# RMSNorm with each row written twice: roots and reciprocals of several rows in one instruction, the last copies on ScalarE

## The chip, the cores and the metric

The kernel runs on one core of a Trainium2 chip. A core has several engines that work side by side, each with its own queue of instructions: VectorE (DVE in the profile), ScalarE (ACT), GpSimd (POOL) and SyncE (SP), which here only issues transfers. TensorE is not used. Sixteen DMA engines move data between the main memory (HBM) and the on-chip memory, whose 128 partitions each hold a stretch of bytes. The metric is device time in microseconds (us); lower is better.

## The reference

```
x_rep = np.repeat(x, 2, axis=1)
rms = np.sqrt((x_rep ** 2).mean(axis=-1, keepdims=True) + 1e-6)
x_norm = x_rep / rms
return (x_norm * gamma[None, None, :]).astype(np.float32)
```

`x` is 8 x 512 x 2048 in float32, 33.6 MB, and `gamma` has 2048 elements. Each of the 4096 rows is divided by the root of its mean square, multiplied by `gamma`, and written twice, one copy after the other: 67.1 MB of output.

## The kernel before

The 4096 rows are cut into eight tiles of 512 rows: a tile has K = 4 rows in each of 128 partitions. One load (`load`, line 50) brings two tiles, that is eight consecutive rows of 8 KB per partition, 8.39 MB. One store (`store`, line 53) writes one tile with every row twice, again eight rows per partition and 8.39 MB. There are four loads and eight stores, all issued by SyncE on one queue, so a store that still waits for its data holds back whatever is behind it.

One buffer `y` holds 24 rows per partition and is used as three areas of eight rows, `first`, `second` and `third`. The function `four` (line 90) works through four tiles and is called twice:

- Load n goes into rows 4 to 11 (half of `first` and half of `second`), load n + 1 into `third`.
- Tile 1 lies in the upper half of `first`. It is spread over all of `first`, to rows 0, 2, 4 and 6 from the front, and stored.
- Tile 2 lies in the lower half of `second`. It is spread over `second`, last row first, and stored.
- Tiles 3 and 4 lie in `third`. The roots of all their eight rows are taken first. Tile 3 then goes to `first`, once the store of tile 1 has read it; tile 4 is spread over `third`.

For each row, ScalarE squares it and sums the squares (`square`, line 60; the sum comes out of a second, short instruction, the accumulator's read-out), then takes the root of the mean plus `eps` (line 62). VectorE takes the reciprocal (line 67) and multiplies the row by it and by `gamma` into its place (line 68). When the four rows of a tile stand, they are copied to the odd places (`repeat`, line 75): the lower two rows by ScalarE, the upper two by VectorE. In tiles 3 and 4 too, each engine takes one copy.

The order on every engine is the program's order (`manual_schedule`, line 86). `constants` (line 109), called once between the first two loads, issues two transfers of `gamma` from ScalarE's queue, spreads it over the partitions on GpSimd and sets `eps_t` by a memset on VectorE. ScalarE's functions come in sets that have to be loaded before the first use (`ACT_TABLE_LOAD`): the profile shows one load before the first square and one before the first root, and none after.

Around the change the order is set by three things: the landing of loads 0 and 2, after which tile 1's four rows go through ScalarE and VectorE; SyncE's queue, in which the store of tile 1 stands behind the two loads; and the landing of tile 1's store, for which the multiplies of tile 3 wait.

Of the kernel before, what the change touches and what calls it, by code (L numbers as in the profile page):

```python
# [1 line left out]

# [4 lines left out]


@with_exitstack
def kernel(  # L10
    ctx: ExitStack,
    tc: tile.TileContext,
    x: bass.AP,
    gamma: bass.AP,
    out: bass.AP,
):
    nc = tc.nc
    P = nc.NUM_PARTITIONS
    f32 = mybir.dt.float32
    Act = mybir.ActivationFunctionType  # L20
    Alu = mybir.AluOpType

    B, S, D = x.shape
    Bo, So, Do = out.shape
    R = So // S
    assert R == 2 and D == Do and B == Bo and So == S * R
    eps = 1e-6
    inv_d = 1.0 / float(D)


    K = 4
    N = B * S
    ntiles = N // (P * K)
    assert N % (P * K) == 0 and ntiles == 8
    H = 2
    x_t = x.rearrange("b s d -> (b s) d").rearrange("(n p k) d -> n p k d", p=P, k=H * K)
    out_t = out.rearrange("b s d -> (b s) d").rearrange("(n p h j) d -> n h p (j d)", p=P, h=H, j=K * R)

    singles = ctx.enter_context(tc.tile_pool(name="singles", bufs=1))
    rows = ctx.enter_context(tc.tile_pool(name="rows", bufs=1))  # L40
    junk = ctx.enter_context(tc.tile_pool(name="junk", bufs=1, space=bass.MemoryType.PSUM))
    small = ctx.enter_context(tc.tile_pool(name="small", bufs=16))

    y = rows.tile([P, 3 * K * R, D], f32, name="y")
    first, second, third = 0, K * R, 2 * K * R

    def load(n, at):
        nc.sync.dma_start(out=y[:, at : at + H * K, :], in_=x_t[n])  # L50

    def store(n, h, to):
        nc.sync.dma_start(  # L53
            out=out_t[n, h], in_=y[:, to : to + K * R, :].rearrange("p j d -> p (j d)")
        )

    def square(row):
        sq = junk.tile([P, D], f32, name="sq")
        ss = small.tile([P, 1], f32, name="ss")
        nc.scalar.activation(out=sq[:], in_=y[:, row, :], func=Act.Square, accum_out=ss[:])  # L60
        rms = small.tile([P, 1], f32, name="rms")
        nc.scalar.activation(out=rms[:], in_=ss[:], func=Act.Sqrt, scale=inv_d, bias=eps_t[:])  # L62
        return rms

    def scale(row, to, rms):
        rstd = small.tile([P, 1], f32, name="rstd")
        nc.vector.reciprocal(out=rstd[:], in_=rms[:])  # L67
        nc.vector.scalar_tensor_tensor(  # L68
            out=y[:, to, :], in0=y[:, row, :], scalar=rstd[:], in1=gamma_b[:],
            op0=Alu.mult, op1=Alu.mult,  # L70
        )

    def repeat(to, n, copy):
        y_r = y[:, to : to + n * R, :].rearrange("p (k r) d -> p k r d", r=R)
        copy(out=y_r[:, :, 1, :], in_=y_r[:, :, 0, :])  # L75

    def squares(at, order):
        return {k: square(at + k) for k in order}

    def spread(at, to, roots):  # L80
        for k, rms in roots.items():
            scale(at + k, to + R * k, rms)
        repeat(to, K // 2, nc.scalar.copy)
        repeat(to + K, K // 2, nc.vector.tensor_copy)

    ctx.enter_context(tc.manual_schedule())

    up, down = range(K), range(K - 1, -1, -1)

    def four(n, constants):  # L90


        load(n, first + K)
        constants()
        load(n + 1, third)
        spread(first + K, first, squares(first + K, up))
        store(n, 0, first)
        spread(second, second, squares(second, down))
        store(n, 1, second)
        roots = [squares(third + h * K, up) for h in range(H)]  # L100
        spread(third, first, roots[0])
        store(n + 1, 0, first)
        spread(third + K, third, roots[1])
        store(n + 1, 1, third)

    gamma_b = singles.tile([P, D], f32, name="gamma_b")
    eps_t = singles.tile([P, 1], f32, name="eps_t")

    def constants():
        for c0 in (0, D // 2):  # L110
            nc.scalar.dma_start(
                out=gamma_b[0:1, c0 : c0 + D // 2],
                in_=gamma[c0 : c0 + D // 2].partition_broadcast(1),
            )
        nc.gpsimd.partition_broadcast(out_ap=gamma_b[:], in_ap=gamma_b[0:1, :])  # L115
        nc.vector.memset(eps_t, eps)  # L116

    four(0, constants)
    four(2, lambda: None)


# [1 line left out]
_INS = ['x', 'gamma']  # L123
_OUTS = [((8, 1024, 2048), 'float32')]


# [23 lines left out]
```

## Time and profile before

| | |
|---|---|
| median of 3 runs | 239.42 us (239.24 to 239.42) |
| the profiled execution's own time | 239.18 us |
| its span | 237.4 us |
| VectorE busy | 96.4 us, 73 instructions |
| ScalarE busy | 101.2 us, 106 instructions |
| data moved | 100.69 MB, 424 GB/s over the span |
| square, read-out, root (one) | 1864, 186, 294 ns |
| reciprocal, multiply (one) | 158, 2352 ns |
| copy of 128x4096 on ScalarE, on VectorE | 3597, 2292 ns |

The profile is that of one execution. Its span runs from the first to the last recorded instruction and is a little shorter than the execution's time. An "L" with a number is a line of the kernel. Busy time counts an engine's work alone; an engine that is not the limit may be idle for free. The chain of waits is followed back from the last instruction, at each step to what released it.

### The profile page before, as it was taken

The numbers are of one execution on the slowest core, as the hardware profiler recorded it, in microseconds if no ns is written. First come the engines' busy times: TensorE is split into PE (matmuls) and PEld (weight loads), VectorE is DVE, ScalarE is ACT, GpSimd is POOL, SyncE is SP. The second block draws the span as 40 slices with busy tenths as digits, with TensorE's granted clock in tenths as the row PEclk, the third lists the DMA queues.
The fourth block names the chain that finished last, engine by engine and source line by source line (L and its number), as shares of the span: only waits on it lengthen the run. The fifth ranks groups of instructions, "written<-read, shape, count | busy, mean of one in ns | idle before, by whom it ended". The sixth has DMA issues, their size and how long they took to land.

```text
span 237.4 us, 267 instructions
## 1 busy us (share of the span) xinstructions
DVE 96.4 (41%) x73; ACT 101.2 (43%) x106; POOL 2.5 (1%) x5
## 2 busy tenths in 40 slices
DVE  0000599950599950000000019999008999100000
ACT  2002999589993600000000059994999805000000
POOL 0210000000000000000000000000000000000000
DMA  9898989989898999989898989889898989899894
GB/s 354 365 519 353 530 353 364 519 353 530 353 519 366 475 409 431 453 386 497 353 530 353 530 353 497 386 353 531 353 519 364 519 364 508 375 453 431 364 519 177
DMA packets 1735, 100.69 MB, mean 424 GB/s; under 512 B 195, under 2 KB 195, under 8 KB 197
## 3 DMA queue, kind: packets, MB, share of 16 engines
q1 hardware_dynamic: 1728, 100.66, 98.5%
q14 instruction: 3, 0.02, 0.0%
q10 hardware_dynamic: 4, 0.01, 0.0%
HBM read 33.56 MB, written 67.11 MB: 424 GB/s over the span
## 4 chain that ended last, share of the span: by engine, by line
DMA 57%; DVE 14%; ACT 12%; issue 2%; DVEq 0%; SPq 0%
DMA out_dram<-y 31%; DMA y<-in_x_dram 25%; DVE y L68 12%; ACT sq L60 7%; ACT y L75 3%; DVE y L75 2%; ACT rms L62 1%; ACT L62 1%; DVE rstd L67 0%; DVEq L68 0%; SPq L50 0%; SPq L53 0%
## 5 line engine op out<-in xcount | busy, mean ns | idle before, releaser
L60 ACT ACTIVATE sq<-y 128x2048 f32<-128x2048 f32 x32 | 59.7, 1864 | 76.2 <-DMA y<-in_x_dram 76.2
L68 DVE SCALAR_TENSOR_TENSOR y<-y,rstd,gamma_b 128x2048 f32<-128x2048 f32 x32 | 75.3, 2352 | 17.4 <-DMA out_dram<-y 16.3
L67 DVE RECIPROCAL rstd<-rms 128x1 f32<-128x1 f32 x32 | 5.0, 158 | 88.1 <-ACT rms L62 88.0
L75 ACT COPY y<-y 128x4096 f32<-128x4096 f32 x8 | 28.8, 3597 | 19.3 <-DVE y L68 19.3
L75 DVE COPY y<-y 128x4096 f32<-128x4096 f32 x8 | 18.3, 2292 | 0.2
L62 ACT ACTIVATE rms<-ss,eps_t 128x1 f32<-128x1 f32 x32 | 9.4, 294 | 1.0
L60 ACT ACTIVATION_READ_ACCUMULATOR sq<-y 128x1 f32 x32 | 6.0, 186 | 0.0
L115 POOL PARTITION_BROADCAST gamma_b<-gamma_b x1 | 2.3, 2292 | 10.1 <-DMA gamma_b<-in_gamma_dram 10.1
L60 ACT ACT_TABLE_LOAD x1 | 1.3, 1283 | 1.5 <-PEq L134 1.5
L62 ACT ACT_TABLE_LOAD x1 | 1.3, 1283 | 0.0
L116 DVE MEMSET eps_t<- 128x1 f32 x1 | 0.1, 59 | 0.8 <-PEq L134 0.8
L134 POOL MEMSET const-bfloat16-1.0<- 128x1 bf16 x1 | 0.1, 102 | 0.0
L134 POOL MEMSET const-uint8-127<- 128x1 uint8 x1 | 0.1, 101 | 0.0
L134 POOL MEMSET const-float32-0.0<- 128x1 f32 x1 | 0.1, 98 | 0.2 <-issue 0.2
L134 POOL MEMSET const-float32-1.0<- 128x1 f32 x1 | 0.1, 98 | 0.0
## 6 DMA issues: line engine op xcount, KB each, us to landing
out_dram<-y SPq DMA_DIRECT2D x8, 29.2
y<-in_x_dram SPq DMA_DIRECT2D x4, 38.7
gamma_b<-in_gamma_dram ACTq DMA_DIRECT2D x2, 4.0 KB
```

The costliest lines, as they stand in the source:

```text
L60: nc.scalar.activation(out=sq[:], in_=y[:, row, :], func=Act.Square, accum_out=ss[:])
L62: nc.scalar.activation(out=rms[:], in_=ss[:], func=Act.Sqrt, scale=inv_d, bias=eps_t[:])
L67: nc.vector.reciprocal(out=rstd[:], in_=rms[:])
L68: nc.vector.scalar_tensor_tensor(out=y[:, to, :], in0=y[:, row, :], scalar=rstd[:], in1=gamma_b[:], op0=Alu.mult, op1=Alu.mult,)
L75: copy(out=y_r[:, :, 1, :], in_=y_r[:, :, 0, :])
L115: nc.gpsimd.partition_broadcast(out_ap=gamma_b[:], in_ap=gamma_b[0:1, :])
L116: nc.vector.memset(eps_t, eps)
L134: nc = _bacc.Bacc("TRN2", target_bir_lowering=False, num_devices=1)
```

## The change

Three things are changed.

1. Roots and reciprocals are taken of several rows at once. `squares` now squares n rows, each with its sum in one column of a 128 x n tile, and takes one root of that tile; `scale` takes one reciprocal of 128 x n and then multiplies the n rows one after the other. In tile 1 of each group of four n is two, done twice: the second pair is squared after the first pair's root. In tiles 2, 3 and 4 n is four.
2. In tiles 3 and 4 ScalarE makes all copies: tile 3's in two instructions of two rows, tile 4's in one of four rows. In tiles 1 and 2 the work stays divided, except that in tile 2 the two engines swap halves: ScalarE takes the upper half, which with the last row first is finished earlier.
3. In `constants`, ScalarE takes the root of one column of `eps_t` into a tile that nobody reads, ahead of the first square.

The pool `small` keeps 4 buffers of each name instead of 16.

```diff
-    small = ctx.enter_context(tc.tile_pool(name="small", bufs=16))
+    small = ctx.enter_context(tc.tile_pool(name="small", bufs=4))
...
+    def squares(at, rows):
+
+        n = len(rows)
+        ss = small.tile([P, n], f32, name=f"ss{n}")
+        for c, k in enumerate(rows):
+            sq = junk.tile([P, D], f32, name="sq")
+            nc.scalar.activation(
+                out=sq[:], in_=y[:, at + k, :], func=Act.Square, accum_out=ss[:, c : c + 1]
+            )
+        rms = small.tile([P, n], f32, name=f"rms{n}")
         nc.scalar.activation(out=rms[:], in_=ss[:], func=Act.Sqrt, scale=inv_d, bias=eps_t[:])
         return rms
 
-    def scale(row, to, rms):
-        rstd = small.tile([P, 1], f32, name="rstd")
+    def scale(at, to, rows, rms):
+        n = len(rows)
+        rstd = small.tile([P, n], f32, name=f"rstd{n}")
         nc.vector.reciprocal(out=rstd[:], in_=rms[:])
-        nc.vector.scalar_tensor_tensor(
-            out=y[:, to, :], in0=y[:, row, :], scalar=rstd[:], in1=gamma_b[:],
-            op0=Alu.mult, op1=Alu.mult,
-        )
+        for c, k in enumerate(rows):
+            nc.vector.scalar_tensor_tensor(
+                out=y[:, to + R * k, :], in0=y[:, at + k, :], scalar=rstd[:, c : c + 1],
+                in1=gamma_b[:], op0=Alu.mult, op1=Alu.mult,
+            )
 
-    def repeat(to, n, copy):
-        y_r = y[:, to : to + n * R, :].rearrange("p (k r) d -> p k r d", r=R)
+    def repeat(to, k0, k1, copy):
+        y_r = y[:, to + R * k0 : to + R * k1, :].rearrange("p (k r) d -> p k r d", r=R)
         copy(out=y_r[:, :, 1, :], in_=y_r[:, :, 0, :])
...
-        spread(first + K, first, squares(first + K, up))
+        for rows in (up[:half], up[half:]):
+            scale(first + K, first, rows, squares(first + K, rows))
+        repeat(first, 0, half, nc.scalar.copy)
+        repeat(first, half, K, nc.vector.tensor_copy)
         store(n, 0, first)
-        spread(second, second, squares(second, down))
+        scale(second, second, down, squares(second, down))
+        repeat(second, half, K, nc.scalar.copy)
+        repeat(second, 0, half, nc.vector.tensor_copy)
         store(n, 1, second)
         roots = [squares(third + h * K, up) for h in range(H)]
-        spread(third, first, roots[0])
+        scale(third, first, up, roots[0])
+        repeat(first, 0, half, nc.scalar.copy)
+        repeat(first, half, K, nc.scalar.copy)
         store(n + 1, 0, first)
-        spread(third + K, third, roots[1])
+        scale(third + K, third, up, roots[1])
+        repeat(third, 0, K, nc.scalar.copy)
         store(n + 1, 1, third)
...
+        root = singles.tile([P, 1], f32, name="root")
+        nc.scalar.activation(out=root[:], in_=eps_t[:], func=Act.Sqrt)
```

More of the change, by code (lines that the diff above doesn't have):

```diff
@@ L55, in store @@
         )
[L57 to L61, printed above, removed]
+    def squares(at, rows):
[7 more added lines that the diff above has]
+        rms = small.tile([P, n], f32, name=f"rms{n}")
         nc.scalar.activation(out=rms[:], in_=ss[:], func=Act.Sqrt, scale=inv_d, bias=eps_t[:])
         return rms
-    def scale(row, to, rms):
-        rstd = small.tile([P, 1], f32, name="rstd")
+    def scale(at, to, rows, rms):
+        n = len(rows)
+        rstd = small.tile([P, n], f32, name=f"rstd{n}")
         nc.vector.reciprocal(out=rstd[:], in_=rms[:])
-        nc.vector.scalar_tensor_tensor(
-            out=y[:, to, :], in0=y[:, row, :], scalar=rstd[:], in1=gamma_b[:],
-            op0=Alu.mult, op1=Alu.mult,
-        )
-    def repeat(to, n, copy):
-        y_r = y[:, to : to + n * R, :].rearrange("p (k r) d -> p k r d", r=R)
[L75 to L84, printed above, removed]
+        for c, k in enumerate(rows):
[5 more added lines that the diff above has]
+        y_r = y[:, to + R * k0 : to + R * k1, :].rearrange("p (k r) d -> p k r d", r=R)
+        copy(out=y_r[:, :, 1, :], in_=y_r[:, :, 0, :])
     ctx.enter_context(tc.manual_schedule())
-    up, down = range(K), range(K - 1, -1, -1)
+    half = K // 2
+    up, down = list(range(K)), list(range(K - 1, -1, -1))
     def four(n, constants):
```

## The prediction

> **What bounds the kernel now.** I read the page's header and shares first, then the chain of waits in order of time, the waits of SP's queue, and the timeline of VectorE and ScalarE between each load's landing and the store that follows it.
>
> ```profile
> span 237.4 us, 267 instructions
> ...
> DVE 96.4 (41%) x73; ACT 101.2 (43%) x106; POOL 2.5 (1%) x5
> ...
> DMA  9898989989898999989898989889898989899894
> ...
> q1 hardware_dynamic: 1728, 100.66, 98.5%
> q14 instruction: 3, 0.02, 0.0%
> ```
>
> No engine is half busy, but the one data queue (q1: packets, MB, share) is full from end to end; q14 fetches instructions. Work taken off VectorE or ScalarE is worth nothing by itself. What can move the end is a moment at which the queue has too little behind the transfer it is on. The chain of waits (start, length, what, in us) shows the queue's calendar:
>
> ```profile
> 0.72 21.70 DMA y<-in_x_dram
> ...
> 38.49 23.45 DMA out_dram<-y
> ...
> 74.20 26.38 DMA out_dram<-y
> ...
> 100.67 38.56 DMA y<-in_x_dram
> ...
> 153.94 24.64 DMA out_dram<-y
> ```
>
> Start plus length is a landing. Load 0 lands at 22.42, the first store at 61.94, the third at 100.58, load 2 at 139.23, the fifth store at 178.58; every transfer is 8.39 MB. Two transfers took 39.52, 38.64, 38.65 and 39.35. So one transfer runs 19.32, and the first and last stretches, which alone hold a load with a store behind it, lost 0.88 and 0.70. Without loss load 1 was due at 22.42 + 19.32 = 41.74 and load 3 at 158.55. Their stores were issued 3.25 and 4.61 ahead of that. The store with less lead lost more.
>
> The records of single packets say where: a 64 KB packet takes 2.418 on each of the 16 DMA engines, but the last one of load 1 took 2.73 to 3.31 (mean 0.63 over), and that of load 3 2.42 to 2.92 (mean 0.27 over). The other addition in the last stretch is one packet of 2.776, on the engine that ends last, at 160.8, beside an instruction fetch at 160.5: 0.36, of which 0.34 reaches the end because the next engine finishes 0.34 earlier. So the second loss splits into 0.36 for the change from load to store and 0.34 for the fetch.
>
> What issues these two stores is VectorE's copy, as SP's waits (time, times, longest) say:
>
> ```profile
> SPq L53 <- DVE y L75: 143.2, 8, 36.8
> ...
> SPq L53 <- ACT y L75: 2.8, 2, 1.4
> ```
>
> **The change, part by part.** The chain before the first store (start, length, engine, line):
>
> ```profile
> 22.45 1.88 ACT L60 ACTIVATE sq<-y 128x2048 f32<-128x2048 f32 x1 [19.67 <-DMA y<-in_x_dram]
> 24.27 0.19 ACT L60 ACTIVATION_READ_ACCUMULATOR sq<-y 128x1 f32 x1
> 24.47 1.28 ACT L62 ACT_TABLE_LOAD   x1
> 25.76 0.29 ACT L62 ACTIVATE rms<-ss,eps_t 128x1 f32<-128x1 f32 x1
> ...
> 26.35 2.35 DVE L68 SCALAR_TENSOR_TENSOR y<-y,rstd,gamma_b 128x2048 f32<-128x2048 f32 x1
> ...
> 33.73 2.35 DVE L68 SCALAR_TENSOR_TENSOR y<-y,rstd,gamma_b 128x2048 f32<-128x2048 f32 x1
> ...
> 36.12 2.29 DVE L75 COPY y<-y 128x4096 f32<-128x4096 f32 x1
> ```
>
> *First store.* Spacings from these rows and their neighbours: square to read-out 1.82, read-out to the next ScalarE operation 0.21, root to reciprocal 0.33, reciprocal to multiply 0.26 the first time and 0.19 later, multiply to reciprocal 2.27, multiply to copy 2.39. Multiply directly after multiply has no row; it lies between 2.27 and 2.39, and I take the busy time, 2.35. The table load (1.28) leaves this chain; a second square (2.03) enters ahead of the first root, and one reciprocal of a pair leaves between multiplies. After: squares at 22.45 and 24.48, root 26.51, reciprocal 26.84, multiplies 27.10 and 29.45, second pair's reciprocal 31.72 (its root, at some 30.8, is ready), multiplies 31.91 and 34.26, copy 36.65 to 38.94, store at 39.02. That is 0.53 later than 38.49 (0.37 to 0.61 with the two bounds). ScalarE's copy follows the second multiply at 31.8 and ends at 35.4, covered by VectorE.
>
> *Early table.* The added 128x1 root waits for the memset of `eps_t` (over by 0.85) and sits behind the two gamma issues on ScalarE's queue; table and root end near 3.1, and ScalarE is idle to 22.45. It costs nothing, nor can it delay SP's loads, which wait for neither. All 31 later squares ran without a table load after the root's, so one set holds both. The fifth store gains nothing from it: its chain had no load.
>
> The Trainium skill, "ScalarE: Activation LUTs", section "What ACT_TABLE_LOAD costs", gives about 2.66 us for a switch, drain included. The row goes from the load's start at 24.47 to the root at 25.76, which is 1.29 and no more; by the page's figure the first store would come 0.85 earlier than before, not 0.53 later, and the whole sum below would be about 0.5 us less.
>
> *Fifth store (second group of four tiles).* Before: data 139.25, root 141.29, reciprocal 141.62, multiply 141.81, copy 151.58, store 153.94. After: second square 141.29, root 143.31, reciprocal 143.64, multiplies 143.83 and 146.18, reciprocal 148.45, multiplies 148.64 and 150.99, copy 153.38 to 155.67, store 155.74: 1.80 later (1.64 to 1.88). Here nothing pays for the second square.
>
> *The other six stores.* The four squares now precede one root (4 x 2.02 instead of starting VectorE after one), and ScalarE's 3.60 replaces VectorE's 2.29 for the last two tiles' copies. By the same spacings the second store goes from 52.1 to 55.7, the third from 74.2 to 75.9 (ScalarE squares until 68.9, then two copies of 3.6), the fourth from 86.5 to about 88.5 (one copy of 128x8192, twice 3.60). The queue is busy with earlier stores to 61.9, 81.3 and 100.6, so they still have 6, 5.3 and 12 in hand. Sixth, seventh and eighth likewise: about 172.7, 192.8 and 204.8 against 178.6, 197.9 and 217.2. Stores behind stores with 7.1 in hand lost nothing (the stretch to 100.58 is clean); no row shows one with 5.3, so each of the two could lose between 0 and the 0.36 seen at 4.61. I take 0: the nearest row of its kind is clean. The last store only has to be queued, so the tail after it stays.
>
> *Fewer small instructions.* 21 roots and 22 reciprocals go (6.2 of ScalarE, 3.5 of VectorE, averages of 294 and 158 ns), and 4 of 8 VectorE copies. ScalarE would be busy some 113, VectorE 86, both under the queue. With a shorter program one instruction fetch may vanish: 0 to -0.34; I take 0, since nothing shows whose fetch it is.
>
> **The one price that is unknown: less lead.** First lead falls from 3.25 to 2.72, the other from 4.61 to 2.81 (the shift of the first store moves load 3 and its data alike). Lower bound: the loss is full once the packet behind is late, as at load 1, so the first adds 0 and the second goes from 0.36 to 0.88: +0.52. Straight line through both rows: (0.88 - 0.36) / (4.61 - 3.25) = 0.38 per us; first +0.20, second 0.88 + 0.38 x 0.44 - 0.36 = +0.69; together +0.89. Upper: below the lead of 3.25 every us costs one: +0.53 and +0.96, +1.49. Below the lower bound lies no effect at all, 0. I take +0.7, between the capped value and the line, because the engines' losses at load 1 show no trend among themselves. Sum: the profiled execution's 239.18 (span 237.4) + 0.7 = 239.9; it stands 0.24 under the median of 239.42, so the forecast is **240.1**.
>
> A page speaks the other way. The Trainium skill, "DMA: Bandwidth & Descriptors", section on latency, puts the first byte of a hardware-queued transfer at about 0.6 us. By that, a store issued 2.7 ahead is in time and the sum is 239.4. The rows of 3.25 with 0.88 lost speak against it.
>
> **Rivals.**
> *A. Not slower: direction alone.* The loss belongs to reading giving way to writing, whatever the lead; the load in flight covers both later issues. For it: both places lose, and no place without a direction change does. Against: 0.63 and 0.27 mean, where the direction is the same. Time 239.4; 239.1 if the fetch goes. It decides if both stretches stay under about 39.6.
> *B. Plain starvation.* One for one below 3.25: 239.42 + 1.49 = 240.9. For it: the smaller lead lost more. Against: the slope seen is 0.38.
> *C. The last tiles' copies become the wait.* ScalarE ends its squares late, and its two copies in a row hold the third and seventh store. It decides when they are issued after 81.3 or 197.9, which needs 5 more than worked out; at 0.36 each it would add 0.7 to the forecast: 240.8.
> *D. Faster.* The fetch goes (-0.34) and, with A, the losses at the two places come out at least 0.2 smaller, since they vary from engine to engine: under 238.9.
>
> **How the numbers follow.** A measurement of this kernel can tell 0.2%, 0.48 us. The forecast's case, +0.4 to +1.1, has 0.45 (0.04 of it inside that bound); A 0.37; B 0.11; C 0.03; D 0.04. Slower: 0.41 + 0.11 + 0.03 = 0.55; same: 0.37 + 0.04 = 0.41; faster 0.04. The range of 239.3 to 241.0 reaches into A down to a fetch partly gone and takes in B; the forecast's own range is 239.8 to 240.5.
>
> **What would show it.** Right: first store near 39.0 and fifth near 155.7 plus the first loss; one table load, before 3; first stretch 39.6 to 39.8, last 39.8 to 40.1, the two between at 38.6; third and seventh store released by ScalarE with slack. Wrong: stretches as before although the stores are later (A), a first stretch near 40.1 (B), a clean stretch grown (C), or no instruction fetch beside the slowest engine (D).

## The result, and the profile after

The changed kernel is faster: 238.66 us (238.50 to 238.83, 8 runs) against 239.22 us (239.12 to 239.54, 8 runs). The ratio is 0.9969, with a 95% interval of 0.9959 to 0.9979. The forecast was 240.1, with 239.3 to 241.0 around it: the sign was wrong.

The page of the changed kernel (span; busy time and instructions of each engine; the queues with packets, MB and share):

```profile
span 236.7 us, 218 instructions
...
DVE 84.4 (36%) x47; ACT 110.2 (47%) x86; POOL 2.5 (1%) x5
...
q1 hardware_dynamic: 1728, 100.66, 98.5%
...
q14 instruction: 1, 0.01, 0.0%
```

VectorE lost 12 us of work and ScalarE gained 9, and neither matters: the data queue is as full as before. Of the two instruction fetches that fell into the run before (at 75.5 and 160.5), one is left (at 152.6).

ScalarE, VectorE and SP before the first store (start, length, engine, line; the last row takes four issues together and starts with the first of them):

```profile
1.51 1.28 ACT L126 ACT_TABLE_LOAD   x1 [1.51 <-PEq L144]
...
22.61 1.88 ACT L63 ACTIVATE sq<-y 128x2048 f32<-128x2048 f32 x1 [19.61 <-DMA y<-in_x_dram]
...
26.68 0.30 ACT L67 ACTIVATE rms<-ss,eps_t 128x2 f32<-128x2 f32 x1
...
27.27 4.62 DVE L75 SCALAR_TENSOR_TENSOR y<-y,rstd,gamma_b 128x2048 f32<-128x2048 f32 x2
...
32.00 4.74 DVE L75 SCALAR_TENSOR_TENSOR y<-y,rstd,gamma_b 128x2048 f32<-128x2048 f32 x2
...
36.77 2.29 DVE L82 COPY y<-y 128x4096 f32<-128x4096 f32 x1
...
39.15 48.18 SPq L53 DMA_DIRECT2D out_dram<-y  x4
```

The steps are the ones that the prediction wrote down. The table is in by 2.8; the first root takes two rows; the store goes out at 39.15, 0.66 later than before. In the second group the data are there at 138.68 and the fifth store goes out at 155.14: 16.46 after its data, against 14.69 before.

The queue's calendar, from the chain of waits, and then the wait of tile 3's multiplies for the first store, in the kernel before and in the changed one:

```profile
0.72 21.87 DMA y<-in_x_dram
...
99.98 38.68 DMA y<-in_x_dram
...
155.14 22.72 DMA out_dram<-y
```

```profile
62.07 2.35 DVE L68 SCALAR_TENSOR_TENSOR y<-y,rstd,gamma_b 128x2048 f32<-128x2048 f32 x1 [7.59 <-DMA out_dram<-y]
```

```profile
61.39 9.14 DVE L75 SCALAR_TENSOR_TENSOR y<-y,rstd,gamma_b 128x2048 f32<-128x2048 f32 x4 [0.48 <-DMA out_dram<-y]
```

Load 0 lands at 22.59. Tile 3's multiplies start on the first store's landing at 61.39, against 62.07 before; from tile 1's first square to there it was 39.62 and is 38.78. So 0.84 us were gained at the place where the prediction put its first loss, although the store there was issued later. From there to load 2's data it is 77.29 (77.18 before), and from there to the fifth store's landing 39.30 (39.45). The records of single packets agree. On the mean of the 16 DMA engines the last packet of load 1 was 0.63 over the usual 2.418 and is now 0.03 over. That of load 3, with the one ahead of it, was 0.27 over and is 0.04. A new loss of 0.29 stands at the change from the fourth store to load 2, where before there was 0.01. Followed at each moment on the DMA engine that is last there, these add up to what the end moved: 0.16 later start, -0.85 at load 1, +0.14 at load 2, +0.30 at load 3 (0.29 of it a packet of 2.711 beside an instruction fetch at 152.6), and -0.33 for the packet beside a fetch that the kernel before had after load 3. The sum is -0.58; the last packet ends at 235.46 against 236.03.

So the queue, which was the limit and still is, lost less although two of its transfers were issued with less lead. The question for the runs was why.

### The profile page after: what moved, and what is told of

Read it like the earlier page. It is cut to its first block, busy times and chain, and to the rows that moved or that the text cites. A ratio compares the mean times of both kernels' runs of the same rounds, so it can differ in the third digit from the quotient of the medians.

```text
span 236.7 us, 218 instructions
## 1 busy us (share of the span) xinstructions
DVE 84.4 (36%) x47; ACT 110.2 (47%) x86; POOL 2.5 (1%) x5
## 4 chain that ended last, share of the span: by engine, by line
DMA 45%; ACT 26%; DVE 13%; issue 1%; DVEq 0%; SPq 0%
DMA y<-in_x_dram 26%; DMA out_dram<-y 20%; ACT sq L63 15%; DVE y L75 13%; ACT y L82 11%; ACT rms L67 1%; DVE rstd L73 0%; DVEq L75 0%; SPq L50 0%
## 5 line engine op out<-in xcount | busy, mean ns | idle before, releaser
L75 DVE SCALAR_TENSOR_TENSOR y<-y,rstd,gamma_b 128x2048 f32<-128x2048 f32 x32 | 73.8, 2349 | 2.1 <-DMA out_dram<-y 1.5
L82 ACT COPY y<-y 128x4096 f32<-128x4096 f32 (+1 forms) x10 | 42.6, 4283 | 19.5 <-DVE y L75 19.5
L73 DVE RECIPROCAL rstd<-rms 128x4 f32<-128x4 f32 (+1 forms) x10 | 1.7, 170 | 109.0 <-ACT rms L67 109.0
L82 DVE COPY y<-y 128x4096 f32<-128x4096 f32 x4 | 9.2, 2293 | 0.1
L67 ACT ACTIVATE rms<-ss,eps_t 128x4 f32<-128x4 f32 (+1 forms) x10 | 3.0, 297 | 0.3
```

What stands on the lines that cost most here:

```text
L75: nc.vector.scalar_tensor_tensor(out=y[:, to + R * k, :], in0=y[:, at + k, :], scalar=rstd[:, c : c + 1], in1=gamma_b[:], op0=Alu.mult, op ...
```

## The experiments

"Lead" is again load 0's (or load 2's) landing plus 19.32, less the store's issue. "Loss" is the time by which packets ran over 2.418, on the mean of the 16 engines, from the packet records; "store to load" is the change from the fourth store to load 2. "Empty" is the mean time between two packets, at the first store, at store to load and at the fifth store, where there is any. The last column is the median of the kernel before in the same comparison. Leads, losses and gaps are those of the one profiled execution of each kernel, whose time lies between 0.35 under the median (a_notable) and 0.45 over it (d_later). The table has all runs; the text below goes through them.

| kernel | first store: lead, loss | at store to load: loss | fifth store: lead, loss | empty | median, us | before beside it |
|---|---|---|---|---|---|---|
| before | 3.25, 0.63 | 0.01 | 4.61, 0.27 | 0 | 239.22 | |
| changed | 2.76, 0.03 | 0.29 | 2.84, 0.04 | 0 | 238.66 | 239.22 |
| p_table | 4.53, 1.06 | 0.00 | 4.61, 0.09 | 0 | 239.53 | 239.43 |
| p_tile1 | 2.76, 0.05 | 0.26 | 2.84, 0.01 | 0 | 238.56 | 239.43 |
| p_tile2 | 3.25, 0.45 | 0.06 | 4.61, 0.30 | 0 | 239.25 | 239.43 |
| p_tile34 | 3.25, 0.36 | 0.05 | 4.61, 0.43 | 0 | 239.51 | 239.43 |
| d_late | 2.89, 0.08 | 0.24 | 2.73, 0.01 | 0 | 238.58 | 239.43 |
| d_later | 1.37, 0.00 | 0.79 | 1.34, 0.00 | 0.53, 0.07, 0.96 | 240.08 | 239.43 |
| a_notable | 1.49, 0.00 | 0.91 | 2.84, 0.05 | 0.21, 0.05, 0 | 240.31 | 239.43 |
| a_rows | 4.54, 0.96 | 0.00 | 4.61, 0.30 | 0 | 239.26 | 239.43 |
| d_first | 2.89, 0.02 | 0.27 | 4.62, 0.90 | 0 | 239.51 | 239.34 |
| d_fifth | 3.26, 0.30 | 0.09 | 2.73, 0.00 | 0 | 238.66 | 239.34 |
| d_mid | 2.23, 0.01 | 0.67 | 2.16, 0.11 | 0.08, 0.15, 0.36 | 239.93 | 239.34 |
| a_hold | 2.75, 0.07 | 0.68 | 2.87, 0.01 | 0, 0.11, 0 | 238.96 | 239.34 |
| a_rows_g1 | 4.53, 0.95 | 0.02 | 2.84, 0.02 | 0 | 239.15 | 239.36 |
| a_rows_g2 | 2.77, 0.09 | 0.27 | 4.62, 0.59 | 0 | 239.12 | 239.36 |
| a_hold_3 | 2.76, 0.02 | 0.27 | 2.84, 0.01 | 0 | 238.76 | 239.36 |
| a_hold_5 | 2.77, 0.02 | 0.31 | 2.85, 0.00 | 0 | 238.62 | 239.36 |
| early_7 | 6.94, 1.09 | 0.03 | 7.00, 0.20 | 0 | 239.60 | 239.27 |

### One part of the change at a time

The early table alone:

```diff
+        root = singles.tile([P, 1], f32, name="root")
+        nc.scalar.activation(out=root[:], in_=eps_t[:], func=Act.Sqrt)
```

> The kernel before with the early root of eps_t alone: the table is loaded ahead of the data, so the first store is issued near 37.2 us, not 38.49. Lead (the theory of the prediction: the queue loses time where a store is issued too shortly before the load ahead of it lands): the first loss shrinks from 0.88 by about 0.4, time -0.4 us. VectorE (the queue loses time where VectorE works on tile 2 while the load ahead of the store lands; after the change VectorE was idle there): VectorE starts tile 2 as closely behind as before, so no change within 0.15. Chance (the losses sit where they happen to sit in a program, whatever its parts do): any change up to 0.6 either way.

Measured: 239.53, ratio 1.0002 (0.9993 to 1.0010). The first store went out at 37.60, earlier than ever, and its loss did not shrink; it grew from 0.63 to 1.06. This is the first row against the prediction's theory: more lead, more loss.

The early table and tile 1 in two pairs, the rest as before (`squares_of` and `scale_of` are the changed kernel's `squares` and `scale`, put beside the old ones; their text and the early root are not shown):

```diff
-        spread(first + K, first, squares(first + K, up))
+        for rows_ in (up[: K // 2], up[K // 2 :]):
+            scale_of(first + K, first, rows_, squares_of(first + K, rows_))
+        repeat(first, K // 2, nc.scalar.copy)
+        repeat(first + K, K // 2, nc.vector.tensor_copy)
```

> The kernel before with the early table and tile 1 in two pairs; tiles 2 to 4 as before. First store near 39.1, fifth near 155.7. Lead: +0.7 us, as the prediction had it for the whole change. VectorE: tile 2's reciprocals and multiplies follow at once, so VectorE is busy while loads 1 and 3 land; no change within 0.15. Chance: up to 0.6 either way.

Measured: 238.56, ratio 0.9964 (0.9952 to 0.9977). This part carries all of the gain. "Lead" fails again, with its +0.7. VectorE was busy while load 1 landed, with tile 2's multiply from 39.17 on, so the theory named VectorE falls here too.

Tile 2 alone, and tiles 3 and 4 alone:

```diff
-        spread(second, second, squares(second, down))
+        scale_of(second, second, down, squares_of(second, down))
+        repeat(second + K, K // 2, nc.scalar.copy)
+        repeat(second, K // 2, nc.vector.tensor_copy)
```

> The kernel before with tile 2 alone changed: one root and one reciprocal for its four rows, halves of the copies swapped. First and fifth store are issued as before (38.5 and 153.9). Lead: no change within 0.15. VectorE: VectorE is idle from the end of tile 1's copy (38.4) to about 44, so the first loss of 0.88 goes and most of the second; -0.6 us, the whole gain of the change. Chance: up to 0.6 either way.

```diff
-        roots = [squares(third + h * K, up) for h in range(H)]
-        spread(third, first, roots[0])
+        roots = [squares_of(third + h * K, up) for h in range(H)]
+        scale_of(third, first, up, roots[0])
+        repeat(first, K // 2, nc.scalar.copy)
+        repeat(first + K, K // 2, nc.scalar.copy)
         store(n + 1, 0, first)
-        spread(third + K, third, roots[1])
+        scale_of(third + K, third, up, roots[1])
+        repeat(third, K, nc.scalar.copy)
```

> The kernel before with tiles 3 and 4 alone changed: one root and one reciprocal for four rows, all copies on ScalarE. Nothing moves at the first and fifth store. Lead and VectorE: no change within 0.15 us; the stores of tiles 3 and 4 come 2 us later, still 5 ahead. Chance: up to 0.6 either way.

Measured: 239.25, ratio 0.9992 (0.9984 to 1.0001), and 239.51, ratio 1.0006 (0.9996 to 1.0015). Neither tells from no change. Work on tiles 2 to 4 is off the path. The four kernels also cross the two things that could matter at the first store. With VectorE busy on tile 2 behind it, the loss is 0.63 at 3.25 ahead (before) and 0.05 at 2.76 (p_tile1); with VectorE idle there it is 0.45 at 3.25 (p_tile2, idle from 38.4 to 44.6) and 0.03 at 2.76 (the changed kernel). In these profiles, one for each kernel, the loss goes with the time of the issue, not with VectorE.

### Is it the time of the issue?

p_tile1 changes the work and the time of two issues. The next kernel leaves the work as it was and delays the two issues, and with them what VectorE does behind them: the kernel before, with copies of `gamma_b` into a tile that nobody reads, on VectorE ahead of tile 1's last copy.

```diff
         repeat(to, K // 2, nc.scalar.copy)
+        for w in pads:
+            nc.vector.tensor_copy(out=scratch[:, :w], in_=gamma_b[:, :w])
         repeat(to + K, K // 2, nc.vector.tensor_copy)
...
-        spread(first + K, first, squares(first + K, up))
+        spread(first + K, first, squares(first + K, up), (810,) if n == 0 else (1400, 1400, 180))
```

> The kernel before, with idle copies of gamma_b into a scratch tile on VectorE ahead of tile 1's last copy: 0.5 us in the first group, 1.8 in the second. The two stores are issued about 2.75 and 2.8 us ahead of their load's due landing, as in the changed kernel; nothing else of the change is made. Early (new theory: a store queued behind a load costs the queue more the earlier it is issued, from about 3 us ahead on): -0.6 us or a little more, both losses under 0.1 on the mean engine, against 0.63 and 0.27 before. Work (the gain comes from tile 1's fewer small instructions, not from the time of the issue): no change within 0.15. Lead (the prediction's): +0.7.

Measured: 238.58, ratio 0.9962 (0.9948 to 0.9975). Pure waste in front of two stores gains as much as the whole change, and the theory named Work falls. Its timeline around both issues:

```profile
36.20 0.58 DVE L85 COPY scratch<-gamma_b 128x810 f32<-128x810 f32 x1
36.69 2.29 DVE L75 COPY y<-y 128x4096 f32<-128x4096 f32 x1
...
39.06 0.35 SPq L53 DMA_DIRECT2D out_dram<-y  x1
...
151.23 2.10 DVE L85 COPY scratch<-gamma_b 128x1400 f32<-128x1400 f32 x3
153.24 2.29 DVE L75 COPY y<-y 128x4096 f32<-128x4096 f32 x1
...
155.59 0.34 SPq L53 DMA_DIRECT2D out_dram<-y  x1
```

Longer copies put both stores later still:

```diff
-(810,) if n == 0 else (1400, 1400, 180)
+(1400, 1400, 180) if n == 0 else (1400, 1400, 1400, 1070)
```

> The same with 1.8 us of idle copies in the first group and 3.1 in the second: both stores some 1.5 us ahead of their load's due landing. Early: the loss does not come back by itself, so -0.6 like the shorter delay, unless the store now comes too late, for which about 1.0 us from issue to first packet (load 0: issued 0.72, first packet 1.74) leaves 0.5 in hand. Work: 0. Lead: +1.5 or more.

Measured: 240.08, ratio 1.0027 (1.0015 to 1.0039). Now the store comes too late. No packet is stretched at load 1, but the queue is empty for 0.53 at the first store and 0.96 at the fifth, and the change from store to load loses 0.79. The store issued at 40.86 has its first packets between 41.70 and 42.09, that is 0.84 to 1.23 after the issue; the Trainium skill, "DMA: Bandwidth & Descriptors", section "Latency and other measured facts", gives about 0.6 for the first byte, and the run's number stands. A delay between the two, (1400, 300) and (1400, 1400, 1290):

> The kernel before with 1.05 us of idle copies in the first group and 2.4 in the second, so that both stores are some 2.2 us ahead. Window: neither stretched packets nor an empty queue above 0.3; between the shorter delay's 238.6 and the longer one's 240.1, near 238.9 if the loss at the later store-to-load change grows with the lateness as the two rows had it (0.24 and 0.79 on the mean engine).

Measured: 239.93, ratio 1.0025 (1.0011 to 1.0038). Already with 2.2 ahead the queue has gaps, and with 0.67 lost at store to load it is much nearer to the long delay than to the short one. The expectation of 238.9 was wrong: the window is narrow on its late side. Nothing was run between 2.2 and 2.7 ahead.

### What each part is there for

The changed kernel without the early root:

```diff
-        root = singles.tile([P, 1], f32, name="root")
-        nc.scalar.activation(out=root[:], in_=eps_t[:], func=Act.Sqrt)
```

> The changed kernel without the early root, so that the table load of 1.28 us is back in tile 1's chain of the first group: first store near 40.4, 1.5 us ahead; the fifth stays 2.8 ahead. Early: same as the changed kernel, within 0.15 of 238.7, if 1.5 ahead is soon enough. Lead: +0.5 us against the changed kernel. Work: +0, the table is hidden.

Measured: 240.31, ratio 1.0038 (1.0027 to 1.0050). The load is back in tile 1's chain:

```profile
26.59 1.28 ACT L67 ACT_TABLE_LOAD   x1
27.89 0.30 ACT L67 ACTIVATE rms<-ss,eps_t 128x2 f32<-128x2 f32 x1
```

The first store goes out at 40.35, only 1.49 ahead, and the loss at store to load grows from 0.29 to 0.91. None of the three theories had the size: "Early" held only if 1.5 ahead was soon enough, which it was not, "Lead" gave a third of the 1.65 that were lost against the changed kernel, and "Work" gave nothing. The early table gains nothing alone, and without it the pairs make the kernel slower than before.

The changed kernel with tile 1 by single rows, the table kept:

```diff
-        for rows in (up[:half], up[half:]):
-            scale(first + K, first, rows, squares(first + K, rows))
+        roots = [squares(first + K, [k]) for k in up]
+        for k in up:
+            scale(first + K, first, [k], roots[k])
```

> The changed kernel with tile 1 by single rows again (a root and a reciprocal for each), the early table kept; tiles 2, 3 and 4 as changed. Stores one and five are issued about 4.5 us ahead of their load's due landing. Early: the losses of the kernel with the early table alone come back, 1.06 and 0.1 to 0.4 on the mean engine, and the gain is lost: 239.3 to 239.6. Lead: faster than the changed kernel by 0.3. Work: between the two kernels, about 239.1.

Measured: 239.26, ratio 0.9990 (0.9978 to 1.0003). Both stores are early again (37.47 and 154.36) and most or all of the gain is lost, with losses of 0.96 and 0.30 (1.06 and 0.09 with the early table alone).

### Two losses, or one that is paid once?

The delays of d_late, one at a time:

```diff
-(810,) if n == 0 else (1400, 1400, 180)
+(810,) if n == 0 else ()
```

> The kernel before with the first store alone held back, 0.5 us of idle copies on VectorE; the fifth goes out as before, 4.6 us ahead. Window (theory now: a store behind a load is free only when it is issued some 2 to 3 us ahead of the load's landing; earlier it stretches the load's last packets, later the queue stands empty): the first loss of 0.63 on the mean engine goes, the second of 0.27 stays; -0.5 us, most of the 0.85 that both delays gave.

```diff
-(810,) if n == 0 else (1400, 1400, 180)
+() if n == 0 else (1400, 1400, 180)
```

> The kernel before with the fifth store alone held back by 1.8 us; the first goes out as before, 3.25 ahead. Window: the first loss stays, the second of 0.27 goes; -0.3 us.

Measured: 239.51, ratio 1.0006 (0.9996 to 1.0015), for the first alone, and 238.66, ratio 0.9980 (0.9970 to 0.9989), for the fifth alone. Both differ from what was expected. By the ratios the fifth alone gave about half of what both delays gave (0.9962); its profiled execution (238.57) is one of its fastest. With the first store held the first loss did go, to 0.02, but the fifth store, issued 4.62 ahead as ever, now lost 0.90 where it had lost 0.27. The wait of tile 3's multiplies for the fifth store shows it, first in d_first, then in d_late:

```profile
179.09 2.35 DVE L68 SCALAR_TENSOR_TENSOR y<-y,rstd,gamma_b 128x2048 f32<-128x2048 f32 x1 [9.51 <-DMA out_dram<-y]
```

```profile
178.31 2.35 DVE L68 SCALAR_TENSOR_TENSOR y<-y,rstd,gamma_b 128x2048 f32<-128x2048 f32 x1 [6.87 <-DMA out_dram<-y]
```

In d_first the data of load 2 are there 0.18 earlier (138.84 against 139.02) and the store is issued 2.07 earlier (153.52 against 155.59), and it lands 0.78 later.

The changed kernel with tile 1 by single rows in one group of four tiles only tests the same from the other side:

```diff
-        for rows in (up[:half], up[half:]):
-            scale(first + K, first, rows, squares(first + K, rows))
+        if n == 0:
+            roots = [squares(first + K, [k]) for k in up]
+            for k in up:
+                scale(first + K, first, [k], roots[k])
+        else:
+            for rows in (up[:half], up[half:]):
+                scale(first + K, first, rows, squares(first + K, rows))
```

> The changed kernel with tile 1 by single rows in the first group of four tiles only: first store some 4.5 us ahead of its load's due landing, fifth 2.8 ahead. Once (about 1 us is lost in all, once, if either store is early): 0.9 to 1.1 on the mean engine at the first store, nothing at the fifth; near 239.3. Each (each store has its own loss, which its lead sets): 1.0 at the first, nothing at the fifth, also near 239.3. Fifth (only the fifth store's issue matters to the end, as holding it alone gave most of the gain): 238.7.

With `if n:` in place of `if n == 0:`

> The changed kernel with tile 1 by single rows in the second group only: first store 2.75 us ahead, fifth 4.5. Once: next to nothing at the first store, 0.8 to 1.0 on the mean engine at the fifth; 239.4. Each: nothing at the first, and at the fifth the 0.27 that it lost at this lead before; 238.9.

Measured: 239.15, ratio 0.9989 (0.9979 to 0.9999), and 239.12, ratio 0.9987 (0.9974 to 1.0000). Either early store takes most of the gain away, so "Fifth" falls for the first. In the second the fifth store lost 0.59: more than the 0.27 of "Each", less than the 0.8 to 1.0 of "Once". Its profiled execution took 238.79 and is the fastest of ten, so the typical loss may be larger.

Taken together, the seven fifth stores issued 4.6 ahead fall nearly into a row (one profile each) by what the two earlier changes of direction had already lost: after 0.29 and 0.36 they lost 0.90 and 0.59, after 0.41 and 0.51 they lost 0.43 and 0.30, after 0.64 it was 0.27, after 0.96 and 1.06 it was 0.30 and 0.09. So the losses are not independent. In all three places together 0.8 to 1.3 is lost once a store is 4.5 or more ahead, wherever that is, and 0.3 to 0.4 when both stores sit near 2.8, or the first at 3.26 and the fifth at 2.73 (d_fifth). These are readings of one profile for each kernel; the first store's loss at 3.25 ahead varies in them from 0.30 to 0.63.

Whether an earlier store loses more yet, with tile 1's squares and roots left out: its rows are all divided by one early root of `eps`, so tile 1's output is not the reference's (the lines that make that root are not shown):

```diff
-        spread(first + K, first, squares(first + K, up))
+        spread(first + K, first, {k: root for k in up})
```

> The kernel before with tile 1's squares and roots left out (its four rows are divided by the root of eps instead, so tile 1's output is not the reference's): VectorE starts on tile 1 as soon as load 0 lands, and the first and fifth store go out about 7 us ahead of their load's due landing. Once and full at about 1 us: 0.9 to 1.2 on the mean engine at the first store, 0.1 to 0.3 at the fifth, as with 4.5 ahead; about 239.4. Growing on with the lead: 1.06 + 2.5 x 0.35 (the slope from 3.25 to 4.5), 1.9 at the first store; 240.2.

Measured: 239.60, ratio 1.0015 (1.0006 to 1.0025); 1.09 lost at the first store, 0.20 at the fifth. The loss at the first store is full at about one microsecond; it does not grow with the lead beyond 4.5.

### What is left in the changed kernel

Load 2 held back by idle copies on ScalarE into the rows that it fills; they wait for the third store, as the load does:

```diff
+        if n:
+            for _ in range(2):
+                nc.scalar.copy(out=y[:, first + K : first + 2 * K, :], in_=y[:, first : first + K, :])
+            nc.scalar.copy(out=y[:, first + K, :], in_=y[:, first, :])
+            nc.scalar.copy(out=y[:, first + K, : 800], in_=y[:, first, : 800])
         load(n, first + K)
```

> The changed kernel with load 2 held back from 100 us to about 116.4 by idle copies on ScalarE into the rows that the load fills, 2.9 us ahead of the landing of the fourth store, behind which it stands. Window, if it holds for a load behind a store too: the stretch of 0.29 on the mean engine (0.68 on the last to end) at the change from store to load goes, -0.3 us against the changed kernel, 238.4. If that stretch is a debt of the first change of direction and not of the load's early issue: no change within 0.15, or slower by up to 0.7 if a load needs to be queued earlier than a store.

a_hold_3 leaves out the last copy, a_hold_5 the last two.

> The changed kernel with load 2 held back to about 116.6 us, 3 us ahead of the landing of the store that it stands behind. Load early (the 0.29 on the mean engine at this change comes from a load queued 19 us ahead): the stretch goes and the queue doesn't stand empty, 238.4. Otherwise the first packets of the load take longer, as they did with 2.3 ahead (0.68 on the mean engine): 238.7 to 239.0.

> The same with load 2 issued at about 114.7 us, 5 ahead. Load early: between the row above and the changed kernel, 238.5. Otherwise: the changed kernel's 238.7, with the same 0.3 on the mean engine at this change.

Measured: 238.96, ratio 0.9983 (0.9974 to 0.9993), 238.76, ratio 0.9977 (0.9967 to 0.9987), and 238.62, ratio 0.9965 (0.9950 to 0.9979). The loads were issued at 117.47, 115.98 and 114.16, which is 2.3, 3.2 and 5.2 ahead of the fourth store's landing, and the losses at store to load were 0.68, 0.27 and 0.31, against 0.29 in the changed kernel with 19. The load's early issue is not what costs in sum; "Load early" falls. The packets show that the cost changes its place. With 19 and 5 ahead the last packets of the fourth store run over, by 0.21 and 0.22, and the first packets of load 2 by 0.07 and 0.09. With 3.2 and 2.3 ahead the store's last packets are clean (just as load 1's are once the first store is issued 2.8 ahead), but the load's first packets run over, by 0.27 and 0.68. Nothing was run between 3.2 and 5.2 ahead. No kernel of the study is faster than the changed one by more than the intervals can tell.

## Why the prediction was wrong

- *What bounds the kernel* was right: the data queue, and in it the two places where a store stands behind a load. That work taken off VectorE or ScalarE is worth nothing held (p_tile2, p_tile34). The sums of busy work were off: the prediction's own terms give 83.7 for VectorE and 109.4 for ScalarE, not 86 and 113, and 84.4 and 110.2 were measured.
- *When the two stores are issued* was right: 39.15 against 39.02, the fifth 16.46 after its data against 16.49. So was the early table's place (1.51 to 2.79), and that stores 3 and 7 would be released by ScalarE with slack: they went out 4.5 and 5.1 ahead, and the stretch around them did not grow.
- *"The store with less lead lost more"* is the step that failed, and everything in "The one price that is unknown" rests on it. Two rows, 3.25 with 0.88 and 4.61 with 0.36 (0.63 and 0.27 on the mean engine), were drawn as a line, and less lead was priced at +0.7. They were not two readings of one law: the second was smaller because the first had been paid. With the first loss gone and the fifth store at the same lead, the second rose from 0.27 to 0.90 (d_first) and 0.59 (a_rows_g2). Where nothing is paid before, at the first store, 4.5 ahead costs 0.95 to 1.06 and 3.25 costs 0.30 to 0.63; the sign of the slope is the other way. +0.7 was forecast, and -0.56 measured (medians).
- *The bounds* left the true case out. Below nothing there was no bound at all ("Below the lower bound lies no effect"): that a later issue could gain was excluded without a reason. Rival A's sign came (both stretches under 39.6), but its direction alone does not decide: in the changed kernel reading gives way to writing as before, with 0.03 lost. Rival D, at 0.04, has the right side of the number (238.66 is under its 238.9), but not the reason: it wanted the fetch gone and put smaller losses down to the spread between engines, while the gain comes back in p_tile1 and d_late, which issue both stores later, and about half of it in d_fifth.
- *Rival B*, starvation, is real but begins lower than 3.25. The changed kernel's 2.8 is still free; 2.2 is not (d_mid), and 1.4 costs 1.5 us against 2.8 (240.08 against 238.58).
- *The weighing of the page against the rows.* By the Trainium skill's figure of about 0.6 a store 2.7 ahead was in time, and it was; the rows that spoke against it were misread. The figure does not give the edge, though: an estimate by it would let 1.4 ahead pass as well, and there the queue ran empty (d_later). On the other side the same page's section "Rules for kernel authors" advises to "Issue the DMA early" so that a transfer's fixed setup overlaps with compute. In this full queue the runs differ: 4.5 ahead instead of 2.8 costs 0.7 (a_rows against d_late, 239.26 and 238.58 in one comparison).
- *The fetch.* One instruction fetch during the run remained and met the engine that ends last again (0.29), so the 0.34 did not go.

Why a store that waits behind a load in flight stretches that load's last packets, why the loss is full at one microsecond, and why 0.3 remains at the next change from store to load, no run shows. That cause stays open; what the runs show is that the time of the issue sets the loss.

## What to carry to other kernels

When one queue is the limit, look at each place where its direction changes, and move the issue there both ways before deciding that earlier is better: a few idle copies in front of two stores are a cheap test, and here they were worth the whole change. Two losses read from one trace may not be two readings of the same law; ask whether the first has changed the state in which the second was taken. A part that does nothing alone (the early table, 1.0002) can be what keeps another part from doing harm (1.0038 without it).

## What was not expected of the hardware

- A store queued behind a load in flight stretches the load's packets by less than 0.1 in a narrow window, 2.7 to 2.9 us ahead of the load's due landing; after such a first store 0.24 to 0.31 is then lost at the next change from store to load. At the first store, 3.25 ahead, the load's last packet already runs 0.3 to 0.6 over, and at 4.5 to 7 about 1.0 (2.418 is its usual time). At 2.2 the queue has gaps.
- A load behind a store behaves otherwise: 3.2, 5.2 and 19 us ahead cost the same in sum, 0.3; 2.3 ahead costs 0.7. At 5.2 and 19 it is mostly the store's last packets that run over, at 3.2 and 2.3 the load's first.
- Stores behind stores (issued 3.5 us and more ahead of the landing of the store in front) and loads behind loads (19 us and more) lost at most 0.02 at each change.
- A late first store costs more than half of its price 75 us later: in the profile of a_notable the queue was empty for 0.21 at that store, and the next change from store to load lost 0.62 more than in the changed kernel.
